# The gate-weight casts and the distance table move behind token tile 2 on ScalarE

## The chip, the cores and the metric

The kernel runs on one core of one Trainium2 chip. The metric is the device time of one execution in microseconds (us), given as the median over several executions. Engines are named as in the profile: PE is TensorE's matmul, PEld its weight loads, DVE is VectorE, ACT is ScalarE, POOL is GpSimd, SP is the engine whose queue issues most DMAs.

## What is computed

One encoder layer on a sequence of S = 1024 tokens of width D = 1024, all in float32:

```python
h = rmsnorm(x, g_mix)
z = h @ w_in                         # pooling channels | q | k | v, 8 heads
y_pool = pool_mixer(u_pool, ...)     # windows 2, 4, 8, 16: mean - self, per-group map
y_attn = diff_attention(q, k, v)     # p1 - lam * p2, bias -slope * |i - j|, chunk mask
gates = sigmoid(h @ w_gate + b_gate)
x = x + (gated sum of the two branch projections) @ w_out
x = x + (relu(rmsnorm(x, g_ffn) @ w_up) ** 2) @ w_down      # 4096 wide
```

Two pieces matter here. `h @ w_gate` (1024 x 2048) needs nothing but `h`, so its matmuls can fill PE while head 0 of the attention is being prepared. And the table of distances |i - j| is built once and is first needed by the attention scores.

## The kernel before

**Precision.** Each float32 operand is held as two rounded parts, high and low. `split` makes them: ACT casts the high part (L132) and DVE or POOL subtracts it from the source for the low part (L133). `mm3` then issues three matmuls, high x high, high x low and low x high (L153, L154, L155), so a logical product of 128 rows is three instructions on PE. Everything is a stream of such triples, with transposes between them (L291 for the normed tokens, L498 for q and k, L1162 for the MLP's input).

**The start.** The 1024 tokens are eight tiles t of 128. Each one is loaded (`load_x`, L333), squared and summed on ACT (L280, key `sq`t), scaled on DVE after a power on POOL (L261, L262, L284, tiles `hn`), transposed on PE into two banks `hps_0`, `hps_1` of four blocks each (L291) and split into `hT`, in four pieces kp = 0 to 3: the casts have the keys `T`t kp `h`, the subtracts `T`t kp `l`. So `T21h` and `T23h` are the casts of pieces 1 and 3 of token tile 2. In the rows below, `hT_<half of the tokens>_<0 high, 1 low>_<number>` carries them; numbers 169 to 175 (even ones low) are pieces 0 to 3 of tiles 0 to 3, and 339 to 345 those of tiles 4 to 7. With `hT` of a tile complete, head 0's projection of it runs: 24 matmuls into `z_t` (L153 to L155), whose squares (ACT L473) lead to the q/k norm (DVE L476, POOL L477, DVE L480) and whose v part is split into `V`. Then q and k are transposed (`tk`, L498) and copied out.

**Fill work.** Between these, `gate_step` feeds PE with the gate projection. `gate_cols(c)` (L780 on) takes 128 columns of `w_gate`: `fill_w` loads them in two halves (SP queue, L711, tiles `frgate`), casts them on ACT into `fwgate` (L132) and subtracts on POOL (L133); then 24 matmuls of 512 tokens each make `g`c`_0`, 24 more `g`c`_1`, and ACT adds the bias (`go`, L785) and stores. `distances` makes an integer table on POOL, takes the absolute value on ACT (L414, tile `dist`, 128 x 1024) and masks a corner on POOL (L415). `columns` transposes a few rows of parameters (`cols_ps`, L419) and copies them on DVE (L420, L421).

**What sets the order.** The order of each engine's instructions is fixed when the program is built. A scheduler runs the program in a timing model and appends to each engine whatever is ready there and ranks first; each engine then works through its list in order, and an instruction that has to wait holds up all behind it. By hand, the tables `FIRST_ACT`, `FIRST_DVE` and `FIRST_PE` (L49 to L58) chain some of the first instructions: `in_turn` walks the keys of a table and makes each instruction follow the one before in issue order, without a wait between engines. A key is looked up in `marks`, where `split` and the norm code have entered their instructions.

**The end.** After the output projection, `norm_token` normalises each token tile for the MLP; for the last one the elementwise part is on POOL (L1146 to L1159, tile `y`), and PE transposes it in two banks `hb_0`, `hb_1` (L1162). The up projection begins before that is done. It combines halves of tokens and weights so that fewer products are needed: products `X`, `Y`, `Z`, `W` of sums `AS`, `B`, `BT` (made on DVE, L1074 and L1077, from the weights `wu`, which the SP queue loads, and split on ACT and DVE), copies on ACT into `x` (L1298), `U` (L1325, L1335) and `z` (L1330), and sums `u` on DVE (L1304) that ACT squares (L1305, L1306).

Of the kernel before, what the change touches and what calls it, by code (L numbers as in the profile page):

```python
# [11 lines left out]
AF = mybir.ActivationFunctionType  # L12
# [35 lines left out]
N_GP = 1  # L48
FIRST_ACT = (  # L49
    "sq0 gc0 gc1 w0h w1h w2h T00h w3h w4h T02h T01h w5h w6h T03h w7h "  # L50
    "sq1 sq2 zq00 T10h T12h sq3 T11h sq4 V00h T20h lx T13h T22h T21h T23h zq01 V01h T30h T32h"
)
FIRST_DVE = (
    "hn00 hn01 w2l T00l w3l T02l T01l w6l T03l w7l rs1 hn10 hn11 rs2 zr00 gg lp T10l hn20 hn21 "
    "ls T12l rs3 T11l rs4 V00l qn00 T20l nl T13l T22l hn30 hn31 hn40 hn41 T21l T23l zr01 V01l T30l T32l"
)
FIRST_PE = "z00 tr10"
# [11 lines left out]
def encoder_kernel(  # L69
# [21 lines left out]
    nc = tc.nc  # L91
# [27 lines left out]
    def ut(shape, dt, name):  # L119
        return up.tile(shape, dt, tag="U", name=name)  # L120
# [4 lines left out]
    def f(ap):  # L125
        return ap.bitcast(F32)

    marks = {}

    def split(hi, lo, src, lo_eng=None, key=None):  # L130

        a = nc.scalar.copy(hi, src)  # L132
        b = (lo_eng or nc.vector).tensor_tensor(lo, src, f(hi), op=ALU.subtract)  # L133
        if key:
            marks[key + "h"], marks[key + "l"] = a.ins, b.ins
        return b

    def queue_behind(ins, first):
        tc.add_manual_dep(
            ins, first.name,  # L140
            mybir.DependencyInfo(mybir.DependencyClass.NoSync, mybir.DependencyReason.DATA),
            reason="issue order",
        )

    def in_turn(keys):
        keys = keys.split()
        for a, b in zip(keys, keys[1:]):
            queue_behind(marks[b], marks[a])
# [12 lines left out]
    def fw_tile(shape, name):  # L161
        return wpool.tile(shape, F32R, tag="fw", name=name, bufs=N_FW)
# [4 lines left out]
    def fr_tile(shape, name):  # L167
        return fp.tile(shape, F32, tag="fr", name=name, bufs=N_FR)
# [140 lines left out]
    with ExitStack() as ph:  # L309
# [6 lines left out]
        def s1(shape, dt, name, tag, bufs=1):  # L316
            return sq_pool.tile(shape, dt, tag=tag, name=name, bufs=bufs)
# [90 lines left out]
        dist = s1([P, S], F32, "dist", "dist")  # L408

        def distances():  # L410

            di = ut([P, S], I32, "di")
            nc.gpsimd.iota(di, pattern=[[-1, S]], base=S - P, channel_multiplier=1)
            nc.scalar.activation(dist, di, AF.Abs)  # L414
            nc.gpsimd.memset(dist[0:64, S - 64 : S], MASKED)  # L415

        def columns():
# [259 lines left out]
        for g in range(-2, N + 8):  # L677
            for t in range(4, NT):
                if LX[t] == g:
                    load_x(t)  # L680
            for t in range(1, NT):
                if NX[t] == g:
                    norm_x(t)
            if g == G_DIST:
                distances()
            if g == G_COLS:
                columns()
            gens = {}
            for tok in ORDER:
                if tok not in gens:  # L690
                    i = g - tok[1]
                    gens[tok] = stage(tok[0], i) if 0 <= i < N else iter(())
                here = tc.cur_priority
                if tok[0] in "HR" and i == N - 1:
                    tc.cur_priority += LATE
                next(gens[tok], None)
                if tc.cur_priority > here + LATE // 2:
                    tc.cur_priority -= LATE
            for gen in gens.values():
                for _ in gen:  # L700
                    pass


    for keys in (FIRST_ACT, FIRST_DVE, FIRST_PE):
        in_turn(keys)

    def fill_w(src, c0, name):
        ws = []
        for j in range(2):
            rw = fr_tile([P, 4, P], f"fr{name}_{j}")  # L710
            nc.sync.dma_start(  # L711
                rw, src[j * 512 : (j + 1) * 512, c0 : c0 + P].rearrange("(kk p) c -> p kk c", p=P)
            )
            w = fw_tile([P, 2, 4, P], f"fw{name}_{j}")
            stored["lo"] = split(w[:, 0], w[:, 1], rw, nc.gpsimd).ins
            ws.append(w)
        return ws

# [21 lines left out]
    def pool_group(g):  # L740
        win = WINDOWS[g]
        ws = fill_w(w_in, g * P, f"pool{g}")
        rg = fr_tile([P, P], f"rgrp{g}")
        nc.sync.dma_start(rg, w_pool_grp[g])
# [35 lines left out]
    def gate_cols(c):  # L780
        ws = fill_w(w_gate, c * P, f"gate{c}")
        for th in range(2):
            ps = fill_proj(ws, th, f"g{c}_{th}", spare_bank if c >= G_Z else fill_bank)
            fo = fo_tile(f"go{c}_{th}")
            nc.scalar.activation(fo[:, 0:512], ps, AF.Identity, bias=cols[:, c : c + 1])  # L785
            nc.scalar.dma_start(g_dram[c * P : (c + 1) * P, th * 512 : (th + 1) * 512], fo[:, 0:512])
            yield
# [8 lines left out]
    stored = {}  # L796
# [62 lines left out]
    while gate_step():  # L859
        pass  # L860
    assert not units_left

    vpool = attn.enter_context(tc.tile_pool(name="vpool", bufs=1))
    pb = mix.enter_context(tc.tile_pool(name="pb", bufs=5, space=PSUM))
# [750 lines left out]
```

## Time and profile before

| | |
|---|---|
| median of 3 runs | 1527.21 us (1526.54 to 1527.58) |
| the profiled execution | 1530.36 us, of which the span of the engines 1528.6 us |
| granted TensorE clock, mean | 0.999 |
| PE busy | 1515.5 us, 99% of the span, 7457 instructions |
| PEld, DVE, ACT, POOL busy | 85%, 64%, 50%, 21% of the span |
| mean DMA traffic | 155 GB/s |

The profiled execution took 3.15 us more than the median; 1.76 us of its time lie outside the span. A timeline row reads: start in us, duration of the group in us, engine, line, operation, output and inputs by the program's names, partitions x elements, and how many instructions the row joins; in square brackets the engine's idle time before it and what ended that. Matmuls are pipelined, so the time that one costs is read from start to start, not from its duration. A windows row gives a stretch, its length, each engine's busy time with the number of instructions, the granted clock as a fraction (PEclk), the busy share of the DMA engines and GB/s.

### The profile page before, as it was taken

What the parts mean: (1) busy time and instruction counts of PE and PEld (TensorE: products, weight loads), DVE (VectorE), ACT (ScalarE), POOL (GpSimd) and SP (SyncE); (2) the same over time, 40 slices, a digit from 0 to 9 for tenths busy, and PEclk for the clock granted to TensorE, in tenths of its full rate; (3) what the DMA queues carried; (4) which work ended last, traced back from release to release, by engine and by line L of the source; (5) the groups of instructions that cost most, each with busy time, mean ns of one, the idle gap of its engine ahead of it and who ended that gap; (6) DMA issues with size and microseconds to landing.
All of it is one profiled execution on the core that took longest, in us unless ns stands there. A gap on an engine that the chain in (4) does not pass through costs nothing.

```text
span 1528.6 us, 21995 instructions
## 1 busy us (share of the span) xinstructions
PE 1515.5 (99%) x7457; PEld 1306.0 (85%) x7457; DVE 979.3 (64%) x2071; ACT 757.6 (50%) x1567; POOL 325.6 (21%) x413
## 2 busy tenths in 40 slices
PE   8999999999999999999999999999999999999999
PEld 6999999999999999888888887888888888888887
DVE  6666566667666666646578569666665668556572
ACT  6545455545454454454464456555555634333331
POOL 5677433334344342212100120000000000000000
PEclk9999999999999999999999999999999999999999
DMA  7455323223232342727366634454433799537650
GB/s 233 125 167 166 105 63 87 68 82 89 68 92 77 90 131 70 248 89 240 133 213 208 226 117 148 153 181 152 142 134 111 268 326 403 172 124 262 227 193 28
DMA packets 195163, 237.36 MB, mean 155 GB/s; under 512 B 13974, under 2 KB 124523, under 8 KB 195052
## 3 DMA queue, kind: packets, MB, share of 16 engines
q1 hardware_dynamic: 177642, 208.66, 42.2%
q10 hardware_dynamic: 17410, 27.31, 4.7%
q8 instruction: 59, 0.97, 0.3%
q14 instruction: 52, 0.43, 0.1%
HBM read 157.24 MB, written 61.90 MB: 143 GB/s over the span
## 4 chain that ended last, share of the span: by engine, by line
PE 93%; DVE 2%; DMA 2%; ACT 1%; SPq 1%; issue 0%; ACTq 0%; DVEq 0%
PE z L153 6%; PE z L155 6%; PE z L154 6%; PE g L154 4%; PE g L155 4%; PE g L153 4%; PE Da L153 4%; PE Da L154 4%; PE Da L155 4%; PE Db L154 3%; PE Db L155 3%; PE Db L153 3%; PE X L153 2%; PE X L155 2%; PE X L154 2%; PE sc L535 2%
## 5 line engine op out<-in xcount | busy, mean ns | idle before, releaser
L153 PE MATMUL z<-wqkv,hT 128*128 128x384 f32 x512 | 176.6, 345 | 2.5 <-ACT hT L132 2.4
L154 PE MATMUL z<-wqkv,hT 128*128 128x384 f32 x512 | 175.6, 344 | 0.0
L155 PE MATMUL z<-wqkv,hT 128*128 128x384 f32 x512 | 174.8, 342 | 0.1
L546 ACT ACTIVATE s<-s,nm 128x256 f32<-128x256 f32 (+7 forms) x128 | 99.5, 778 | 62.2 <-DVE nm L538 61.4
L153 PEld LDWEIGHTS z<-wqkv,hT 128*128 128x128 f32 x512 | 97.6, 191 | 6.0 <-ACT hT L132 3.3
L153 PE MATMUL g<-hT,fwgate 128*128 128x512 f32 x256 | 100.6, 393 | 0.4 <-ACT hT L132 0.4
L155 PE MATMUL g<-hT,fwgate 128*128 128x512 f32 x256 | 101.0, 394 | 0.0
L154 PE MATMUL g<-hT,fwgate 128*128 128x512 f32 x256 | 100.9, 394 | 0.0
L155 PEld LDWEIGHTS z<-wqkv,hT 128*128 128x128 f32 x512 | 97.4, 190 | 2.8 <-DVE hT L133 0.6
L154 PEld LDWEIGHTS z<-wqkv,hT 128*128 128x128 f32 x512 | 97.6, 191 | 2.2
L477 POOL TENSOR_TENSOR ms<-ms,mhalf 128x4 f32<-128x4 f32 x64 | 69.2, 1081 | 138.3 <-DVE ms L476 137.8
L538 DVE CUSTOM_DVE_ANT_0 s<-sc,dist 128x512 f32<-128x512 f32 (+3 forms) x128 | 73.9, 584 | 38.4 <-PE sc L536 38.2
L133 DVE TENSOR_TENSOR AT<-ta,AT 128x256 fp32r<-128x256 f32 (+1 forms) x160 | 61.2, 392 | 47.8 <-ACT AT L132 47.4
L132 ACT CAST AT<-ta 128x256 fp32r<-128x256 f32 (+1 forms) x160 | 54.1, 349 | 50.0 <-PE ta L578 32.4
L133 DVE TENSOR_TENSOR AS<-s,AS 128x512 fp32r<-128x512 f32 x64 | 45.0, 704 | 37.7 <-ACT AS L132 37.6
L535 PE MATMUL sc<-K,Q 128*128 128x512 f32 (+2 forms) x192 | 68.1, 357 | 0.3 <-DMA Q<-Q 0.3
L536 PE MATMUL sc<-K,Q 128*128 128x512 f32 (+2 forms) x192 | 65.7, 347 | 0.0
L133 POOL TENSOR_TENSOR wqkv<-rqkv,wqkv 128x384 fp32r<-128x384 f32 x60 | 62.0, 1051 | 8.5 <-ACT wqkv L132 7.6
L133 POOL TENSOR_TENSOR fwgate<-frgate,fwgate 128x512 fp32r<-128x512 f32 x32 | 42.7, 1336 | 68.8 <-ACT fwgate L132 58.7
L153 PEld LDWEIGHTS g<-hT,fwgate 128*128 128x128 f32 x256 | 48.1, 188 | 8.9 <-ACT hT L132 0.7
L155 PEld LDWEIGHTS g<-hT,fwgate 128*128 128x128 f32 x256 | 48.1, 188 | 8.7
L154 PEld LDWEIGHTS g<-hT,fwgate 128*128 128x128 f32 x256 | 48.1, 188 | 8.5
(472 smaller groups left out, 4379.8 us busy)
## 6 DMA issues: line engine op xcount, KB each, us to landing
wd<-in_w_down_dram SPq DMA_DIRECT2D x56, 512.0 KB, 5.7
wu<-in_w_up_dram SPq DMA_DIRECT2D x32, 512.0 KB, 4.6
udS<-us SPq DMA_DIRECT2D x64, 256.0 KB, 2.1
ur<-udS SPq DMA_DIRECT2D x32, 512.0 KB, 3.4
rqkv<-in_w_in_dram SPq DMA_DIRECT2D x64, 192.0 KB, 2.7
ud<-u ACTq DMA_DIRECT2D x48, 256.0 KB, 3.0
ur<-ud SPq DMA_DIRECT2D x24, 512.0 KB, 7.3
frgate<-in_w_gate_dram SPq DMA_DIRECT2D x32, 256.0 KB, 2.7
```

Of the source, the lines that this page charges most:

```text
L132: a = nc.scalar.copy(hi, src)
L133: b = (lo_eng or nc.vector).tensor_tensor(lo, src, f(hi), op=ALU.subtract)
L153: nc.tensor.matmul(ps, lhs_hi, rhs_hi, start=first, stop=False, **kw)
L154: nc.tensor.matmul(ps, lhs_hi, rhs_lo, start=False, stop=False, **kw)
L155: return nc.tensor.matmul(ps, lhs_lo, rhs_hi, start=False, stop=last, **kw).ins
L477: nc.gpsimd.tensor_tensor(ms, ms, mhalf[:, 0:4], op=ALU.pow)
L535: nc.tensor.matmul(dst, Q[:, 1, i, :], rhs, start=True, stop=False)
L536: nc.tensor.matmul(dst, Q[:, 0, i, :], rhs, start=False, stop=True)
L538: nc.vector.tensor_tensor_reduce(out=s[i][:, c : c + w], in0=sc[:, 0:w], in1=dist[:, o0 + c : o0 + c + w], scale=2.0 ** -(h + 1), scalar=B ...
L546: nc.scalar.activation(s[i][:, 0:n], s[i][:, 0:n], AF.Exp, bias=last, scale=-1.0, accum_out=Z[:, i, t : t + 1])
```

## The change

Two keys become known to the table of ACT: the absolute value of the distance table gets `di`, and the two casts of a gate's weight columns get `gate`c`0h` and `gate`c`1h` (and the subtracts on POOL `...l`, which no table uses). In `FIRST_ACT`, `di` is put behind `T23h`, and the two casts of the first gate columns behind `zq01`, the squares of `z_1`. Since the gate steps create their instructions later in the program text than the tables were applied, the loop over `in_turn` moves behind them.

```diff
@@ -48,7 +48,7 @@
 FIRST_ACT = (
     "sq0 gc0 gc1 w0h w1h w2h T00h w3h w4h T02h T01h w5h w6h T03h w7h "
-    "sq1 sq2 zq00 T10h T12h sq3 T11h sq4 V00h T20h lx T13h T22h T21h T23h zq01 V01h T30h T32h"
+    "sq1 sq2 zq00 T10h T12h sq3 T11h sq4 V00h T20h lx T13h T22h T21h T23h di zq01 gate00h gate01h V01h T30h T32h"
 )
@@ -411,7 +411,7 @@
             nc.gpsimd.iota(di, pattern=[[-1, S]], base=S - P, channel_multiplier=1)
-            nc.scalar.activation(dist, di, AF.Abs)
+            marks["di"] = nc.scalar.activation(dist, di, AF.Abs).ins
@@ -701,9 +701,6 @@
-    for keys in (FIRST_ACT, FIRST_DVE, FIRST_PE):
-        in_turn(keys)
-
     def fill_w(src, c0, name):
@@ -712,7 +709,7 @@
             w = fw_tile([P, 2, 4, P], f"fw{name}_{j}")
-            stored["lo"] = split(w[:, 0], w[:, 1], rw, nc.gpsimd).ins
+            stored["lo"] = split(w[:, 0], w[:, 1], rw, nc.gpsimd, f"{name}{j}").ins
@@ -859,6 +856,9 @@
     assert not units_left
+
+    for keys in (FIRST_ACT, FIRST_DVE, FIRST_PE):
+        in_turn(keys)
```

**ACT at the start.** The difference of ACT's list where the tables apply; a row with a minus stands there before, one with a plus now. `fwgate_0`, `fwgate_1` are the two halves of the first gate weights, `hps_0_294` and `hps_1_304` the transposed token tile 2.

```order
 L132 CAST hT_0_0_173<-hps_1_304 128x2x128
+L132 CAST hT_0_0_171<-hps_0_294 128x2x128
+L132 CAST hT_0_0_175<-hps_1_304 128x2x128
+L414 ACTIVATE dist<-di 128x1024
+L473 ACTIVATE sq<-z_1_449 128x4x64
 L132 CAST fwgate_0_6508<-frgate_0_6506 128x512
 L132 CAST fwgate_1_6513<-frgate_1_6511 128x512
-L414 ACTIVATE dist<-di 128x1024
-L132 CAST hT_0_0_171<-hps_0_294 128x2x128
-L132 CAST hT_0_0_175<-hps_1_304 128x2x128
-L473 ACTIVATE sq<-z_1_449 128x4x64
 L132 CAST V_0_377<-z_1_449 128x128
```

The casts `T21h` and `T23h`, the distance table and the squares of `z_1` have changed places with the two gate casts.

**PE before the second half of the tokens.** The scheduler, which follows from that order, places the gate products otherwise. Before, the end of `g_0` stands between `z_3` and the transposes that lead to `z_4`:

```order
L154 MATMUL g_0_6516<-hT_0_1_176,fwgate_1_6513 128x512
L155 MATMUL g_0_6516<-hT_0_0_175,fwgate_1_6513 128x512
L291 MATMUL hps_1_564<-identf,hn_547 128x128 x4
L498 MATMUL tk_0_513<-identf,qn_0_446 128x128 x2
L291 MATMUL hps_0_554<-identf,hn_547 128x128 x4
L153 MATMUL z_4_662<-wqkv_0_207,hT_1_0_339 128x384
```

In the changed program `z_3` and one small transpose stand there:

```order
L154 MATMUL z_3_598<-wqkv_7_230,hT_0_0_175 128x384
L155 MATMUL z_3_598<-wqkv_7_230,hT_0_1_176 128x384
L419 MATMUL cols_ps<-identf,rows 128x32
L291 MATMUL hps_1_564<-identf,hn_547 128x128 x4
L498 MATMUL tk_0_513<-identf,qn_0_446 128x128 x2
L291 MATMUL hps_0_554<-identf,hn_547 128x128 x4
L153 MATMUL z_4_662<-wqkv_0_207,hT_1_0_339 128x384
```

All 24 products of `g_0` now stand between `z_2` and `z_3`, where they were mixed with `z_3` and with transposes before. The number of instructions on PE is the same. On DVE, `hn_547` and what follows it to the subtract `T61l` (row `hT_1_1_342<-hps_0_481`) are the same eight steps in another order.

**The beginning of the MLP.** Two places of the late program move too. On PE the two groups of transposes of the last token tile go further back, the first behind five products, the second behind seven; five products stand between them, where there were three. This is the first of the two:

```order
-L1162 MATMUL hb_0_10099<-identf,y_9835 128x128 x4
 L154 MATMUL X_10159<-B11l,A_1_10161 128x512
 L155 MATMUL X_10159<-B11h,A_1_10161 128x512
 L153 MATMUL X_10159<-B11h,A_1_10161 128x512
-L1162 MATMUL hb_1_10100<-identf,y_9835 128x128 x4
 L154 MATMUL X_10159<-B11l,A_1_10161 128x512
 L155 MATMUL X_10159<-B11h,A_1_10161 128x512
+L1162 MATMUL hb_0_10099<-identf,y_9835 128x128 x4
```

Both banks have moved away from the place at which PE met them, and the products passed over need only weights and tokens that were there.

And on ACT, some 25 us later, the copies `U_0` and `z_0` come ahead of the cast of a weight tile that is still being loaded (`A_5`):

```order
 L132 CAST A_4_10698<-wu_0_10694 128x512
-L132 CAST A_5_10858<-wu_0_10854 128x512
 L132 CAST AS_1_10500<-s_1_10460 128x512
-L132 CAST A_1_10523<-wu_1_10454 128x512
 L1325 COPY U_0_10358<-X_10116 128x512
 L1330 COPY z_0_10376<-Z_10360 128x512
+L132 CAST A_5_10858<-wu_0_10854 128x512
+L132 CAST A_1_10523<-wu_1_10454 128x512
```

Before, the copy `U_0` stood behind that cast. Nothing in the diff touches this part of the program: the scheduler's choices there follow from its whole run.

## The prediction

> **What bounds the kernel now.** I read the page's busy times first, then the waits of PE, then the timelines around the places where the order changed.
>
> ```profile
> span 1528.6 us, 21995 instructions
> PE 1515.5 (99%) x7457; PEld 1306.0 (85%) x7457; DVE 979.3 (64%) x2071; ACT 757.6 (50%) x1567; POOL 325.6 (21%) x413
> ...
> PE z L153 <- ACT hT L132: 2.4, 2, 1.6
> PE hb L1162 <- POOL y L1159: 2.0, 2, 1.0
> PE X L153 <- ACT U L1325: 0.9, 1, 0.9
> PE g L153 <- ACT hT L132: 0.4, 1, 0.4
> ```
>
> PE is busy for all but 13.1 us of the span, so the bound is its list of instructions. A change that adds and removes no work there can bring only what PE waits, what a lower clock costs, and what the order of unlike instructions costs. The four waits shown (total, number, longest) are those that stand near a changed row; they sum to 5.7 us. Three are in the rows that follow, with their places.
>
> **The start: what is removed.** ACT's timeline, then PE's, around the first gate casts:
>
> ```profile
> 24.78 1.37 ACT L132 CAST fwgate<-frgate 128x512 fp32r<-128x512 f32 x2 [3.05 <-DMA frgate<-in_w_gate_dram]
> 26.06 1.05 ACT L414 ACTIVATE dist<-di 128x1024 f32<-128x1024 int32 x1
> 27.02 0.62 ACT L132 CAST hT<-hps 128x256 fp32r<-128x256 f32 x2
> ```
> ```profile
> 24.82 1.03 PE L291 MATMUL hps<-identf,hn 128*128 128x128 f32 x8
> 27.43 0.45 PE L153 MATMUL z<-wqkv,hT 128*128 128x384 f32 x1 [1.58 <-ACT hT L132]
> ...
> 28.41 0.50 PE L153 MATMUL g<-hT,fwgate 128*128 128x512 f32 x1 [0.36 <-ACT hT L132]
> ...
> 30.28 0.52 PE L153 MATMUL z<-wqkv,hT 128*128 128x384 f32 x1
> 30.60 0.52 PE L154 MATMUL z<-wqkv,hT 128*128 128x384 f32 x1
> ```
>
> ACT stands 3.05 us on the load of the gate weights, although the casts `T21h` and `T23h`, behind it in its list, read a bank that PE had filled long before. They run at 27.02, after 1.37 of gate casts and 1.05 of the distance table, and PE idles 1.58 and then 0.36 for them. In the new order both casts run in ACT's idle time, from about 21.8, the distance table and the squares of `z_1` fill some more of the 3.05, and the gate casts still start at 24.78 when their load lands. PE's 1.58 + 0.36 = 1.94 us fall away. The low parts of these pieces come from DVE, which is busy to 25.2 with the norm of tiles 3 and 4 and then free, in time for 25.85, when PE's transposes end.
>
> Behind that gap the clock falls:
>
> ```profile
> 25.74:29.15 3.41, 1.47 (x9) 0.96 (x8) 1.75 (x6) 3.41 (x9) 3.41 (x5) 1.00 0.92 348
> 29.15:32.57 3.42, 3.42 (x14) 3.42 (x13) 2.66 (x8) 2.85 (x8) 2.13 (x4) 0.54 0.46 139
> 916.54:919.95 3.41, 2.25 (x11) 1.27 (x10) 3.41 (x6) 2.38 (x5) 3.41 (x2) 1.00 0.10 38
> ```
>
> The window after the gap has a granted clock of 0.54, and products of 384 columns follow each other by 0.32 us (30.28, 30.60) where at full clock it is 0.18 (37.40 and 37.58, quoted next). Over 3.42 us that is 3.42 x (1 - 0.175/0.32) = 1.55 for products alone, and 1.70 with the group of transposes that straddles the end. A window like the third, with PE busy for 2.25 of 3.41, kept its clock; the first, with 1.47, did not. With the gap gone, the first has PE full, so I take the clock to stay up and **1.70** back (bounds 0 and 1.70).
> The Trainium skill ("TensorE: Matmul & The Clock Gate", on the HAM clock gate and its oscillation) has the clock halved after an idle window of about 3.4 us and says "no PE-idle gaps >~3.4µs"; as worded, 1.58 idle would not do it, and the 1.70 would stay. The rows disagree with the letter of it: a gap of less than half that stands right before the only 0.54 here. I keep the other way as rival C.
>
> **The order of groups.** Transposes cost more than themselves:
>
> ```profile
> 36.79 0.60 PE L291 MATMUL hps<-identf,hn 128*128 128x128 f32 x4
> 37.14 0.42 PE L155 MATMUL z<-wqkv,hT 128*128 128x384 f32 x1
> 37.40 0.34 PE L153 MATMUL z<-wqkv,hT 128*128 128x384 f32 x1
> 37.58 0.34 PE L154 MATMUL z<-wqkv,hT 128*128 128x384 f32 x1
> ```
>
> The first product behind a group takes 0.26 from start to start, the others 0.18, so each change of kind costs about 0.09. Between `z_2` and `z_4` the list now has 4 places with transposes where there were 9; 5 x 0.09 = **0.45**. Gross gain at the start: 1.94 + 1.70 + 0.45 = 4.1.
>
> **The start: what is added.** Without the products of `g_0` between `z_3` and the second half's first transposes, what these need is due earlier:
>
> ```profile
> 39.01 1.06 ACT L280 ACTIVATE hn<-x 128x1024 f32<-128x1024 f32 x1
> ...
> 41.08 1.42 DVE L284 SCALAR_TENSOR_TENSOR hn<-x,rs,gmb 128x512 f32<-128x512 f32 x2 [0.19 <-POOL rs L262]
> ...
> 43.88 0.74 DVE L133 TENSOR_TENSOR hT<-hps,hT 128x256 fp32r<-128x256 f32 x2
> ...
> 46.92 0.44 PE L153 MATMUL z<-wqkv,hT 128*128 128x384 f32 x1
> ```
>
> From the start of `hn_547` to the end of `T61l` DVE takes 41.08 to about 44.3, 3.2 us without a pause, for the same steps as in the new order, and `hn_547` starts 2.07 behind its square (39.01). In the new order that square stands behind the casts of tile 5's transposes, which PE reaches after 6 of `z_3`'s 24 products. PE would end `z_3` at about 45.5 - 4.1 = 41.4; counted back (24 products of 0.175, four groups of 0.35), those transposes end near 37.1, the casts near 37.8, so `hn_547` starts near 39.9 and `T61l` ends near 43.1. The transposes in `hps_0` need it, since it empties their bank, and PE would be there at 42.0: a new wait of **1.1**. `z_4` then needs the bank that `qn_2` empties, two DVE steps of about 0.37 behind `T61l`, at 43.9, where PE comes at 43.7: **0.2**. Both are estimates, 1.3 together; 0.3 if the square comes a us earlier than worked out, 2.0 if it comes 0.7 later, since DVE's chain then moves with it.
>
> One more load comes due earlier, the tokens of tile 4 (SP's issue, ACT's square of that tile, and the time to landing of such loads):
>
> ```profile
> 23.33 1.01 SPq L333 DMA_DIRECT2D x<-in_x_dram  x2
> ...
> x<-in_x_dram SPq DMA_DIRECT2D x4, 512.0 KB, 4.3
> ```
> ```profile
> 29.54 1.09 ACT L280 ACTIVATE hn<-x 128x1024 f32<-128x1024 f32 x1
> ```
>
> Issued at 23.33 and with a median of 4.3, it lands between 27.6 and the 29.54 at which it was used. Pulled ahead on ACT, the square may stand there for it, and the casts of tile 3 behind it, whose products PE wants next: 0 to 0.6, I take **0.3**. The net gain at the start is 4.1 - 1.1 - 0.2 - 0.3 = **2.5**; bounds 0.8 (half clock stays) and 3.8 (no `T61l` wait).
>
> **The MLP's beginning.** PE, then ACT:
>
> ```profile
> 918.45 0.66 PE L1162 MATMUL hb<-identf,y 128*128 128x128 f32 x4 [1.00 <-POOL y L1159]
> ...
> 919.17 0.39 PE L155 MATMUL X<-B11h,A 128*128 128x512 f32 x1
> 919.39 0.40 PE L153 MATMUL X<-B11h,A 128*128 128x512 f32 x1
> 920.76 0.66 PE L1162 MATMUL hb<-identf,y 128*128 128x128 f32 x4 [0.97 <-POOL y L1159]
> ...
> 947.32 0.50 PE L153 MATMUL X<-BT3h,AS 128*128 128x512 f32 x1 [0.94 <-ACT U L1325]
> ```
> ```profile
> 945.12 0.62 ACT L132 CAST A<-wu 128x512 fp32r<-128x512 f32 x1 [3.19 <-DMA wu<-in_w_up_dram]
> ...
> 946.69 0.57 ACT L1325 COPY U<-X 128x512 f32<-128x512 f32 x1
> ```
>
> POOL's pieces `y` are ready at 918.45 and 920.76. From start to start the two waits cost 1.17 and 1.14 above a product of 0.227, together 2.3. With five products ahead of the first transposes (5 x 0.227 = 1.14) PE comes to them at 918.4, no wait; five more between the groups bring it to the second at about 920.1, 0.7 early. So 2.3 - 0.7 = **1.6** come back. Later, `U_0` stands behind a cast that waits 3.19 for a weight load; ahead of it, it can be done by about 942.5, two us before PE wants its bank, and **0.9** come back. Against that, `Z_1` now waits on a DVE sum (`u`) that is at the end of a full queue; I take **-0.2**. Net 2.3. The lower bound is 0, from the same DVE:
>
> ```profile
> 910.00:930.00 20.00, 18.03 (x85) 14.49 (x84) 19.98 (x31) 14.03 (x28) 7.63 (x5) 1.00 0.42 131
> 930.00:950.00 20.00, 19.06 (x85) 15.44 (x84) 19.54 (x32) 12.89 (x24) 0.00 (x0) 1.00 0.44 133
> ```
>
> It is busy for 39.5 of these 40 us, so PE, coming earlier, may find the operands that DVE makes not there, and wait for them instead. Two things speak for most of the gain all the same: PE waits for no DVE result in this stretch before, and DVE's own list starts a little earlier there. The upper bound is 2.9, with 0.3 of the second wait left and none on `u`: 2.3 - 0.3 + 0.9.
>
> **Sum.** 2.5 + 2.3 = 4.8. On the profiled execution that is 1528.6 - 4.8 = 1523.8 for the span, or 1525.6 with the 1.76 outside it. That execution lies 3.15 above the median; the waits and the clock are taken to be alike in the timed ones, so the median becomes 1527.21 - 4.8 = **1522.4**.
>
> **The rivals.** *B, only the start pays* (1527.21 - 2.5 = 1524.7): DVE, full over the 40 us, sets the MLP's beginning, and the waits at L1162 and on `U` return as waits for `AS` or `u`. For it the two windows; against it that PE's only waits there name POOL and ACT. *C, the half clock is not the gap's* (4.8 - 1.7 = 3.1, 1524.1): it comes at a time of its own, or the new wait of 1.1 + 0.2 near 42 brings another. For it that one occurrence proves no cause; against it that 1.3 is less than the 1.94 of the window that lost the clock. *D, slower*: the second gate columns.
>
> ```profile
> 26.77 8.73 SPq L711 DMA_DIRECT2D frgate<-in_w_gate_dram  x4
> ```
> ```profile
> 31.29 0.62 ACT L132 CAST fwgate<-frgate 128x512 fp32r<-128x512 f32 x1 [0.57 <-DMA frgate<-in_w_gate_dram]
> ```
>
> Their load is issued when POOL has released a buffer, and landed at 31.29. The cast of it now stands ahead of the squares of `z_2`, a `V` and the casts of tile 4, on which the transposes of `z_3`'s stretch hang. It holds PE up only if it lands later than about 36.5, each us beyond that costs one, and the gain of the start and the end is spent at 41.3; to lose 3.8 it has to land near 45, giving 1531. The buffer's release hangs on the gate casts, which keep their time at 24.78, so 5 us are to spare; against D. *E, no change* (1527): the late choices of the scheduler cancel and the start's gain turns into the wait at `T61l`.
>
> **How the numbers follow.** A measurement of this kernel tells about 0.2%, 3 us, from no change. The forecast with both places has 0.58, B 0.14, C 0.14, D 0.08, E 0.06. Within the forecast the gain is 3.1 to 6.5, nearly always over 3 (0.55 of the 0.58); of B 0.03 and of C 0.04 are over it. Faster 0.62; same 0.03 + 0.11 + 0.10 + 0.06 = 0.30; slower 0.08. The range runs from 1520.0 (all upper bounds but some of the new waits) to 1526.5 (B or C with the start at its lower side), leaving out D, half of E and the rims.
>
> **What would show it.** In PE's waits the rows `z <- ACT hT` and `X <- ACT U` are gone and `hb <- POOL y` is one wait of about 0.7; a wait for a DVE `hT` (L291) of about 1 us appears near 42. The window at 29.15 has a clock of 1.00. ACT's gate casts still start near 24.8, and `z_4` starts near 44.3 instead of 46.92. In the stretch of the MLP's beginning PE comes 2.3 nearer. The prediction is wrong if half clock shows up again between 25 and 50, if PE waits on `AS` or `u` behind 920 for over a us, or if `z_3` waits for a cast behind the gate load.

## The result and the profile after

The changed kernel takes 1524.15 us (median of 19 runs, 1523.14 to 1525.55), the kernel before in the same sessions 1527.38 us (19 runs, 1526.04 to 1529.48). The ratio is 0.9977 with a 95% interval of 0.9971 to 0.9983: 3.5 us faster (2.6 to 4.4), at the edge of what a measurement here tells from no change. Forecast were 1522.4 in a range of 1520.0 to 1526.5, and a gain of 4.8 us, which lies outside 2.6 to 4.4. The spans of the two profiled executions differ by exactly those 4.8 (1528.6 and 1523.8), which is no confirmation: the profiled execution of the kernel before took 1530.36, 3.0 us above its median, that of the changed one 1525.54, 1.4 above.

The waits of the changed kernel's PE (total, how often, the longest):

```profile
PE hps L291 <- DVE hn L284: 1.2, 1, 1.2
PE z L153 <- ACT hT L132: 0.8, 1, 0.8
PE Db L153 <- ACT w_0h L132: 0.6, 1, 0.6
PE hps L291 <- DVE hT L133: 0.5, 1, 0.5
PE hb L1162 <- POOL y L1159: 0.5, 1, 0.5
PE X L155 <- DVE AS L133: 0.2, 1, 0.2
```

The first two stand at the very start, ahead of the changed rows (the second profile of the kernel before, below, has both). Gone are the 1.58 and 0.36 on `hT` at 27 us and the 0.94 on `U`; the two waits on `y` have become one of 0.5. New are 0.5 on `hT` L291, which is the bank that `T61l` empties, 0.2 on `AS`, and 0.6 on `w_0h`, far behind the change at 1258 us.

ACT at the start of the changed kernel (timeline), then PE there, then the two windows after the first token tiles, each with its busy times in the order PE, PEld, DVE, ACT, POOL and its granted clock in the third column from the end:

```profile
22.86 1.06 ACT L414 ACTIVATE dist<-di 128x1024 f32<-128x1024 int32 x1
25.08 0.38 ACT L473 ACTIVATE sq<-z 128x256 f32<-128x256 f32 x1 [1.16 <-PE z L155]
25.36 1.13 ACT L132 CAST fwgate<-frgate 128x512 fp32r<-128x512 f32 x2
```
```profile
25.17 1.47 PE L291 MATMUL hps<-identf,hn 128*128 128x128 f32 x12
26.40 0.42 PE L155 MATMUL z<-wqkv,hT 128*128 128x384 f32 x1
...
42.90 0.66 PE L291 MATMUL hps<-identf,hn 128*128 128x128 f32 x4 [0.53 <-DVE hT L133]
43.56 0.44 PE L153 MATMUL z<-wqkv,hT 128*128 128x384 f32 x1
```
```profile
25.74:29.15 3.41, 3.41 (x26) 3.38 (x25) 1.66 (x6) 3.41 (x9) 3.10 (x3) 1.00 0.54 201
29.15:32.57 3.42, 3.42 (x18) 2.91 (x17) 3.14 (x7) 3.29 (x12) 3.42 (x6) 1.00 0.39 114
```

ACT no longer waits for the load: by 25.36 the weights are there, and what it waits for is `z_1`, whose squares stand ahead of the gate casts now. So these start 0.6 us later than before (24.78) and not at the same time, as was forecast; the first product that needs them comes at 29.71. PE runs without a pause from `z_1` into `z_2`, the clock stays at 1.00, and `z_4` starts at 43.56 instead of 46.92.

The beginning of the MLP in the changed kernel's timeline, PE and then ACT:

```profile
914.62 0.66 PE L1162 MATMUL hb<-identf,y 128*128 128x128 f32 x4
...
916.93 0.66 PE L1162 MATMUL hb<-identf,y 128*128 128x128 f32 x4 [0.51 <-POOL y L1159]
...
941.25 0.39 PE L153 MATMUL X<-BT3h,AS 128*128 128x512 f32 x1
```
```profile
938.57 0.57 ACT L1325 COPY U<-X 128x512 f32<-128x512 f32 x1
...
941.68 1.14 ACT L132 CAST A<-wu 128x512 fp32r<-128x512 f32 x2 [2.04 <-DMA wu<-in_w_up_dram]
```

The first transposes meet a finished `y`, the second wait 0.51, and `U` is copied two us before its bank is wanted, ahead of the cast that waits for `wu`. Taking PE's instructions of the two traces in list order, the changed kernel is ahead by 3.4 us at `z_4`, 3.8 before the MLP, 5.9 at 955 us, and 4.8 from 1265 us to the end: 1.1 are lost again at `w_0h`.

### The profile page after: what moved, and what is told of

Read it like the earlier page. It is cut to its first block, busy times and chain, and to the rows that moved or that the text cites. A ratio compares the mean times of both kernels' runs of the same rounds, so it can differ in the third digit from the quotient of the medians.

```text
span 1523.8 us, 21991 instructions
## 1 busy us (share of the span) xinstructions
PE 1513.8 (99%) x7457; PEld 1304.2 (86%) x7457; DVE 980.4 (64%) x2071; ACT 757.3 (50%) x1567; POOL 327.6 (21%) x413
## 3 DMA queue, kind: packets, MB, share of 16 engines
q1 hardware_dynamic: 177642, 208.66, 42.4%
## 4 chain that ended last, share of the span: by engine, by line
PE 92%; DVE 3%; DMA 2%; ACT 1%; issue 1%; POOL 0%; SPq 0%; ACTq 0%; DVEq 0%; POOLq 0%
PE z L153 6%; PE z L155 6%; PE z L154 6%; PE g L155 4%; PE g L154 4%; PE g L153 4%; PE Da L153 3%; PE Da L154 3%; PE Da L155 3%; PE Db L154 3%; PE Db L155 3%; PE Db L153 3%; PE X L155 2%; PE X L153 2%; PE X L154 2%; PE sc L536 2%
## 5 line engine op out<-in xcount | busy, mean ns | idle before, releaser
L486 POOL TENSOR_TENSOR qn<-qn,ggh 128x128 f32<-128x128 f32 x64 | 33.7, 526 | 105.8 <-DVE qn L480 89.1
L155 PEld LDWEIGHTS g<-hT,fwgate 128*128 128x128 f32 x256 | 48.1, 188 | 8.8
L154 PEld LDWEIGHTS g<-hT,fwgate 128*128 128x128 f32 x256 | 48.1, 188 | 8.5
```

Of the source, the lines that this page charges most:

```text
L154: nc.tensor.matmul(ps, lhs_hi, rhs_lo, start=False, stop=False, **kw)
L155: return nc.tensor.matmul(ps, lhs_lo, rhs_hi, start=False, stop=last, **kw).ins
L486: nc.gpsimd.tensor_tensor(qn[:, :, 1, :], qn[:, :, 1, :], ggh.unsqueeze(1).broadcast_to([P, 2, HD]), op=ALU.mult)
```

## The experiments

All were timed in alternation with the kernel before; each also left a profile. The ratio is to the kernel before of the same session.

| run | what | ratio (95%) |
|---|---|---|
| again | the kernel before | 1.0001 (0.9993 to 1.0010) |
| late_only | only the order of the MLP's beginning | 0.9989 (0.9980 to 0.9998) |
| di_only | only the distance table moved | 0.9995 (0.9987 to 1.0004) |
| gates_only | only the gate casts moved | 0.9974 (0.9964 to 0.9983) |
| start_only | only the order of the start | 0.9989 (0.9980 to 0.9998) |
| load_later_before | before, gate load later | 1.0039 (1.0026 to 1.0051) |
| load_later_after | changed, gate load later | 0.9989 (0.9980 to 0.9998) |
| load_early | before's start, gate load earlier, changed end | 0.9980 (0.9971 to 0.9989) |
| after_again | the changed kernel | 0.9971 (0.9960 to 0.9982) |
| t61_early | changed, `T61l` earlier | 0.9973 (0.9963 to 0.9983) |

### The kernel before, once more

Nothing is edited.

> The kernel before, unchanged, timed against itself and profiled once more. In the two profiles at hand the change is worth 4.8 us, in the timed medians 3.2 us, and the profiled execution of the kernel before was 3.0 above its median. Theory 1 (the half clock at 29 us comes only in some executions of the kernel before, since the clock's windows start at another moment in each): this profile may well show a granted clock of 1.0 behind the gap; then z_4 starts near 45.2 instead of 46.9 and the profiled time lies near the median, 1527 to 1528.5. Theory 2 (it comes in every execution, and the 1.6 us between profile and median are something else): the half clock is there again and z_4 starts at 46.9. The ratio is 1.000 within 0.0006 by both.

Its PE in the timeline, then the window that holds the gap:

```profile
25.76 0.44 PE L153 MATMUL z<-wqkv,hT 128*128 128x384 f32 x1
26.04 0.34 PE L154 MATMUL z<-wqkv,hT 128*128 128x384 f32 x1
26.75 0.50 PE L153 MATMUL g<-hT,fwgate 128*128 128x512 f32 x1 [0.37 <-ACT hT L132]
27.87 0.63 PE L291 MATMUL hps<-identf,hn 128*128 128x128 f32 x4 [0.62 <-DVE hT L133]
...
44.54 0.45 PE L153 MATMUL z<-wqkv,hT 128*128 128x384 f32 x1
```
```profile
26.05:29.46 3.41, 2.42 (x14) 1.82 (x14) 3.26 (x8) 2.88 (x7) 3.01 (x5) 1.00 0.71 229
```

No half clock, and not even the gap of 1.58: PE idles 0.37 + 0.62, and `z_4` starts 2.4 us earlier than in the first profile of the same program. The reason stands on ACT:

```profile
23.12 1.38 ACT L132 CAST fwgate<-frgate 128x512 fp32r<-128x512 f32 x2 [1.25 <-DMA frgate<-in_w_gate_dram]
```

The gate load landed 1.7 us earlier than in the first profile (24.78). The earlier load has a price, too: POOL's subtracts of these weights now run at 23.82, beside DVE's norm of tiles 3 and 4, which takes 4.79 us where it took 2.73 in the first profile. The 0.62 is PE's wait for the subtract behind it:

```profile
22.60 4.79 DVE L284 SCALAR_TENSOR_TENSOR hn<-x,rs,gmb 128x512 f32<-128x512 f32 x4
```

So both the size of the gap and the half clock belong to the execution, not to the program. That is theory 1.

### Only the beginning of the MLP

```diff
+    X1, Y1 = marks["X1"], marks["Y1"]
+    seq = X1[11:] + hb7[:4] + Y1[:5] + hb7[4:] + Y1[5:6]
+    for a, b in zip(seq, seq[1:]):
+        queue_behind(b, a)
+    queue_behind(marks["A11_5h"], marks["z5_0"])
```

`X1` and `Y1` are the twelve products of `X_10159` and `Y_10160`, `hb7` the eight transposes of the last tile; a few lines that record them move the helpers' lines by 2 or 3. On PE only the two groups of transposes move; on ACT the cast of `A_5` goes behind the copies, and one subtract of DVE follows it. The changed kernel's lists differ at more places behind these, up to 1035 us, which stay as before here.

> The start is as in the kernel before; only at the beginning of the MLP the order of the change is put in by hand: the two groups of transposes of the last token tile behind the last five products of X and five of Y, and the copies U_0 and z_0 ahead of the cast of A_5. Theory of two separate gains: PE gains 2.2 us between 900 and 950 (the two waits on POOL's y shrink from 2.0 to about 0.5, the wait on U of 0.9 is gone), and the median falls by 2.2, to a ratio of 0.9986, if nothing is given back; by 1.1 (0.9993) if the first products of the down projection's next group (Db on w_0h) wait again for their weight load as they do in the changed kernel. Rival (DVE sets this place): no gain, ratio 1.000, and the waits come back under AS or u. A second thing it tells, as a third profile of the same start: whether the half clock at 29 us is there (theory 2) or not always (theory 1).

The median falls to 1525.97 from 1528.29, the ratio says 1.7 us (0.3 to 3.1). PE's waits of this kernel:

```profile
PE z L155 <- ACT hT L134: 2.3, 2, 1.5
PE X L157 <- DVE A L135: 0.5, 1, 0.5
PE hb L1165 <- POOL y L1162: 0.5, 1, 0.5
```

The waits on `y` are 0.5, that on `U` is gone, and 0.5 on DVE's part of `A` has come. In its trace PE gains 1.9 us on the first profile of before between 900 and 960, where the changed kernel gains 2.1, and nothing is lost at `w_0h`. So the two places named carry nearly all of it, the end's part is real without the start's, and DVE takes a small share of it back, not all. The start of this program is that of the kernel before, a third profile of it; PE's row at the gap, then the two windows around it:

```profile
25.80 0.45 PE L155 MATMUL z<-wqkv,hT 128*128 128x384 f32 x1 [1.47 <-ACT hT L134]
```
```profile
23.02:26.43 3.41, 1.94 (x13) 1.34 (x11) 1.51 (x4) 3.13 (x8) 2.55 (x3) 1.00 0.99 351
26.43:29.85 3.42, 3.05 (x19) 2.95 (x20) 2.66 (x9) 2.71 (x7) 2.67 (x5) 1.00 0.75 246
```

Here the gap is nearly as long as in the first (1.47 + 0.37, against 1.58 + 0.36), and yet the clock stays: the boundary of the clock's windows falls between the two parts, and neither of the two windows has PE busy for less than 1.94. The gap is long although the load landed as early as in the second profile:

```profile
23.18 1.36 ACT L134 CAST fwgate<-frgate 128x512 fp32r<-128x512 f32 x2 [2.75 <-DMA frgate<-in_w_gate_dram]
```

PE came sooner, with the transposes of tile 3 at 23.30 instead of 24.93, since its full clock began 3 us earlier in this execution (last section). The gap is as long as the load is late against PE, and both vary.

### One part alone

Against the table of the changed kernel, on the first line:

```diff
-    "... T21h T23h di zq01 gate00h gate01h V01h T30h T32h"
+    "... T21h T23h di zq01 V01h T30h T32h"              (di_only)
+    "... T21h T23h zq01 gate00h gate01h V01h T30h T32h" (gates_only)
```

> Only the distance table goes behind T21h and T23h; the gate casts stay ahead of them. The beginning of the MLP keeps the order of the kernel before. ACT makes T21h at 26.05 instead of 27.02, but PE now has the products that wait for it ahead of tile 3's transposes, so it idles about 1.4 us from 25.0 to 26.4 and comes to the next products 0.4 to 0.5 us earlier than before. If the clock falls behind a gap by where the windows lie, 1.4 us in one piece cost 1.7 or nothing: gain 0.5 where the kernel before had full clock, 2.2 where it had half. Median 1526.9 to 1525.2, ratio 0.9997 to 0.9986; theory 1 says near the first, theory 2 near the second. Rival (the distance table alone is what matters): 3 us, 0.998.

> Only the gate casts go behind zq01; the distance table stays ahead of T21h. Orders of PE, DVE, POOL and SP are those of the changed kernel; on ACT the table comes two casts earlier, in time that ACT spends idle. Theory: same as the changed kernel, ratio 0.9979, z_4 at 43.6, PE 5.9 ahead of the kernel before near 950, and it is the gate casts alone that carry the change. Rival (both parts are needed): T21h comes a us later, PE idles 0.5 to 1 us near 26 and the gain falls to 2.2 or less. It is also a second profile of the changed order: if the 1.1 us that were given back at the first Db near 1258 hang on the landing of single loads, the wait for w_0h there may be another (0 to 1.2); if they hang on the order, it is 0.6 again and PE's lead falls from 5.9 to 4.8.

gates_only is the whole change: 0.9974. With its table go the changed lists of PE, DVE, POOL and SP, the end's included; di_only keeps the end of the kernel before. di_only is 0.9995, not told from no change; its PE idles 0.35 at 24.74, because the load landed at 23.04 in this execution too. The expectation of 1.4 there was made for the late load of the first profile. In this one trace `z_4` starts at 43.00, no later than in the changed kernel; the end's waits are those of before. That the distance table alone is worth 3 us is excluded.

In gates_only there is no wait on `w_0h`, though its end has the changed order, and di_only has one of 0.5 with the order before.

### The start alone

From here on every engine's list is written out as a chain of issue order, without waits of its own, so that only what is named differs:

```diff
         encoder_kernel(tc, *args)
+        _in_this_order(nc, tc)
```

> Every engine's list is written out: up to the middle of the program it is that of the changed kernel, from there on (the beginning of the MLP and all behind it) that of the kernel before. Theory of two separate gains, with the half clock left out: the start gives 1.0 to 1.9 (PE's idle time at 26 us was 1.0 in the second profile of the kernel before and 1.9 in the first, less 0.5 for the new wait on T61l, plus about 0.5 of other things in head 0), the MLP's beginning nothing; ratio 0.9990 (0.9987 to 0.9994), waits on POOL's y 2.0 and on U 0.9 as before. If the half clock sat in most executions of the kernel before: 0.9978. If the start gives nothing: 1.000.

Measured 0.9989, as forecast without the half clock, and 0.9978 would be the forecast with it in most executions. Its waits at the end are those of the kernel before:

```profile
PE hb L1162 <- POOL y L1159: 2.0, 2, 1.0
PE X L153 <- ACT U L1325: 1.3, 1, 1.3
```

start_only and late_only together make 0.9989 x 0.9989 = 0.9978, the change 0.9977: two gains of about 1.7 us each that add, as far as intervals of 0.0009 to either side can tell.

### The load later, in both orders

```diff
-frgate_0, frgate_1, wq_0 (2 pieces), x_406, x_408
+wq_0 (2 pieces), x_406, x_408, frgate_0, frgate_1
```

(SP's list of loads; all else as named.)

> All lists are those of the kernel before, but on SP the two loads of the first gate columns go behind four others (two pieces of a branch weight and two token tiles), so they are issued about 2.5 us later. Theory (in the order before, PE's gap at 26 us is as long as the load is late, since T21h and T23h stand behind it on ACT): the gap grows by 2.4 to 3 us to about 4, z_4 starts 2.4 to 3 later, and a half clock of one window (1.7) becomes likely. Ratio 1.0016 to 1.0030. Rival (the gap hangs on something else, such as the distance table or DVE): less than 1 us, ratio 1.000.

> The same delay of the same loads, with all other lists as in the changed kernel. Theory (the changed order takes PE off that load): ACT waits 1 to 2 us for the load near 25.5, but PE has z_2 to do until 29.5; loss against the changed kernel 0 to 0.5, ratio to the kernel before 0.9977 to 0.9982. Rival (whoever needs the gates waits as long as the load is late): 2.4 us, ratio 0.9993.

In the order before, ACT, PE, and the windows around the gap:

```profile
27.86 1.36 ACT L132 CAST fwgate<-frgate 128x512 fp32r<-128x512 f32 x2 [6.80 <-DMA frgate<-in_w_gate_dram]
```
```profile
30.49 0.69 PE L153 MATMUL z<-wqkv,hT 128*128 128x384 f32 x1 [5.35 <-ACT hT L132]
```
```profile
24.25:27.66 3.41, 0.90 (x9) 0.66 (x7) 0.27 (x1) 0.00 (x0) 0.00 (x0) 1.00 0.81 276
27.66:31.07 3.41, 0.58 (x2) 0.50 (x2) 0.60 (x2) 3.08 (x8) 2.52 (x3) 0.50 0.04 12
31.07:34.49 3.42, 3.42 (x12) 2.83 (x11) 2.66 (x8) 3.42 (x10) 2.82 (x6) 0.50 0.53 155
```

ACT and with it DVE and POOL stand still (0.27 and 0.00 of 3.41), PE idles 5.35 us in one piece, and two windows run at half clock. The kernel loses 6.0 us (4.0 to 7.8), more than the 2.4 to 4.6 expected, since the load landed 4.7 later than in the second and third profile, not 2.5.

In the changed order, with the same delay, ACT and PE:

```profile
27.21 1.37 ACT L132 CAST fwgate<-frgate 128x512 fp32r<-128x512 f32 x2 [3.29 <-DMA frgate<-in_w_gate_dram]
```
```profile
29.07 0.49 PE L153 MATMUL g<-hT,fwgate 128*128 128x512 f32 x1 [0.73 <-ACT hT L132]
31.96 0.50 PE L153 MATMUL g<-hT,fwgate 128*128 128x512 f32 x1 [1.00 <-ACT hT L132]
```

The loss is 1.8 us against the change (0.9989 instead of 0.9977; by the two intervals 0.2 to 3.5), where 0 to 0.5 were expected and 2.4 by the rival. In the trace PE waits 0.73 + 1.00, and not for the weights: `g_0` takes all 512 tokens of the first half, and the casts of token tile 3 stand behind the gate casts on ACT. The changed order has put more of PE's work between itself and the load; it has not made PE independent of it.

### The load earlier

```diff
-rqkv_0 (2 pieces), rqkv_1 (2 pieces), frgate_0, frgate_1
+frgate_0, frgate_1, rqkv_0 (2 pieces), rqkv_1 (2 pieces)
```

The lists of the start are those of the kernel before, those of the end the changed ones.

> The start's lists are those of the kernel before, ACT's included, the lists from the MLP's beginning on those of the changed kernel; on SP the loads of the first gate columns go ahead of four weight loads of the next head, so they are issued 2 to 3 us earlier. Theory (the cause is the load's lateness, the order of ACT is one cure of two): the wait of ACT on the load is gone, PE's idle time at 26 us falls under 0.4, z_4 starts near 43.5 without the new wait on T61l, and with the 2.2 of the MLP's beginning the kernel is as fast as the changed one or up to 0.5 faster: ratio 0.9977 (0.9973 to 0.9982). Rival (the order of PE's products at the start is what helps, by fewer changes between transposes and products): it stays at the 2.2 of the end, 0.9986.

0.9980, within what was expected; the end alone (late_only) has 0.9989, and the interval of 0.9971 to 0.9989 holds the rival's 0.9986 too. ACT waits for no gate load any more, but a wait stands in the gap's place all the same (ACT, then PE):

```profile
21.34 1.19 ACT L132 CAST fwgate<-frgate 128x512 fp32r<-128x512 f32 x2
```
```profile
27.96 0.63 PE L291 MATMUL hps<-identf,hn 128*128 128x128 f32 x4 [1.77 <-DVE hT L133]
```

DVE is late. Its work ahead of that `hT` is four `hn` steps, here beside POOL's subtracts of the gate weights and a product behind them (1.17 us); the first row is DVE, the second POOL:

```profile
22.21 5.27 DVE L284 SCALAR_TENSOR_TENSOR hn<-x,rs,gmb 128x512 f32<-128x512 f32 x4
```
```profile
22.37 3.43 POOL L133 TENSOR_TENSOR fwgate<-frgate,fwgate 128x512 fp32r<-128x512 f32 x2
```

In the first profile of the kernel before, and in the changed one, DVE does the same four ahead of the gate casts, while POOL subtracts nothing (changed kernel):

```profile
22.48 2.73 DVE L284 SCALAR_TENSOR_TENSOR hn<-x,rs,gmb 128x512 f32<-128x512 f32 x4
```

5.27 against 2.73, so the earlier load swaps one wait for another of 1.77, and `z_4` starts at 44.63, where 43.5 was expected. The gap has two causes, then: a late load holds `T21h` on ACT, as theory has it, and an early one brings POOL's subtracts beside DVE's norm and so holds the low parts on DVE (0.62 in the second profile of the kernel before). The order of ACT takes both away: with the gate casts behind `z_1`, the four `hn` steps take 2.73 to 2.89 in all six profiles that have this order. In time the two cures are not told apart, nor is the rival (fewer changes between transposes and products) excluded as a part of the start's gain: the early load makes 0.9980 / 0.9989 = 0.9991 beside the end's part, the order of ACT 0.9989 (start_only).

### The changed kernel again, and its one new wait

```diff
 ACT   hT_1_0_343<-hps_1_491
-      sq<-z_3, V_0<-z_3, hT_1_0_341<-hps_0_481
+      hT_1_0_341<-hps_0_481, hT_1_0_345<-hps_1_491, sq<-z_3, V_0<-z_3
 DVE   cols
-      ms_3, V_0, gs, T61l, hT_1_1_344<-hps_1_564, qn_2, T63l
+      T61l, qn_2, T63l, ms_3, V_0, gs, hT_1_1_344<-hps_1_564
```

(t61_early; after_again has no edit.)

> The changed kernel, once more. Ratio to the kernel before 0.9977 within 0.0009. Its second profile shows what is of the order and what of one execution: the wait for T61l (0.5) and one wait on POOL's y (0.5) are there again and no half clock; if the wait for w_0h at 1258 (0.6, with which PE's lead fell from 5.9 to 4.8) is a matter of how single loads land, it may be missing as it was in two other runs with this order of the end; if it is of the order, it is there again.

> All lists are those of the changed kernel, but on ACT the casts T61h and T63h go ahead of the squares of z_3 and its V, and on DVE the subtract T61l and qn_2 go ahead of ms_3, V and gs. Theory (the one wait that the change added at the start, 0.53 for T61l and some 0.2 behind it, is only the order of those small steps): T61l ends at 42.2 instead of 42.8, the wait of the transposes in hps_0 is under 0.1, z_4 starts near 43.0 instead of 43.56, and the kernel is 0.5 to 0.7 us faster than the changed one: ratio to the kernel before 0.9973, which the timing alone can hardly tell from 0.9977. Rival (hn_547's own lateness holds PE there): z_4 does not move.

after_again measured 0.9971. It has the same 0.53 at `T61l` and the same 0.5 on `y`, and no wait on `w_0h`: PE's lead over the first profile of the kernel before is 6.8 us at 960 us and 6.7 at the end, where it fell to 4.8 in the first profile. (1.4 of the 6.7 it had already at the transposes of tile 3, from an earlier full clock.) That loss belonged to one execution.

PE of t61_early, timeline:

```profile
42.24 0.66 PE L291 MATMUL hps<-identf,hn 128*128 128x128 f32 x4
42.75 0.44 PE L498 MATMUL tk<-identf,qn 128*128 128x128 f32 x2
43.20 0.66 PE L291 MATMUL hps<-identf,hn 128*128 128x128 f32 x4
43.71 0.44 PE L153 MATMUL z<-wqkv,hT 128*128 128x384 f32 x1
```

From the first transposes to `z_4` it is 1.47 us, in the changed kernel 41.42 to 43.56, 2.14: the wait is gone and 0.67 with it, by a reordering of small steps alone. In the same execution PE waited 1.1 for `g_0`, so `z_4` itself was late. The gate weights were there; this time the squares of token tile 4 held up the casts of tile 3 on ACT:

```profile
29.74 1.06 ACT L280 ACTIVATE hn<-x 128x1024 f32<-128x1024 f32 x1 [2.09 <-DMA x<-in_x_dram]
```

In after_again ACT waited 1.13 for the same tokens, without a wait of PE; in the first profile of the changed kernel it did not wait. The median (0.9973) cannot show 0.7 us, and whether t61_early beats the changed kernel is left open.

## Why the prediction was right, and which of its terms was not

**Sign, place and both mechanisms held.** ACT's wait for the gate load is what held `T21h` back: moved later, the load costs the old order 6.0 us and the new one 1.8; moved earlier, ACT's wait is gone. And the end's part comes from the two moved groups of transposes and the moved copies: late_only has it without the start.

**The mis-sized term is the clock's 1.70**, "with the gap gone ... I take the clock to stay up and 1.70 back". It was there in one of three profiles of the kernel before's start. Every fall of the clock that was seen followed a gap of PE, but not every such gap brought one: it matters how much of the gap falls into one window of the clock. The granted clock of the first profile rises at 15.74 us, falls at 29.39 and rises at 32.81: four windows of 3.41 and one. The last window before the fall, the one behind it, and a window of load_early:

```profile
25.98:29.39 3.41, 1.60 (x9) 1.20 (x10) 1.94 (x6) 3.41 (x9) 3.41 (x5) 1.00 0.91 345
29.39:32.81 3.42, 3.42 (x12) 3.36 (x11) 2.70 (x7) 2.85 (x9) 2.13 (x4) 0.50 0.41 123
25.74:29.15 3.41, 1.64 (x12) 1.36 (x11) 3.41 (x8) 2.48 (x5) 1.87 (x4) 1.00 1.00 352
```

In the first profile PE was busy for 1.60 of 3.41, and the next window ran at half. With 0.90 and 0.58 (load_later_before) the clock fell or stayed down; with 1.94 (late_only), 2.42 (again) and 1.64 (load_early, 1.77 idle in one piece) it stayed up. So the limit lies near 1.6 by this measure. It is not shown that PE's busy time is exactly what counts: the ends of matmuls are modelled, 1.60 and 1.64 are close, and the last window of late_only (1518.06 to 1521.47), also with 1.60, was followed by no fall. The windows lie differently in each execution (the first rise is at 12.78 to 15.81 us in the twelve traces), so a gap of 1.8 us costs half a window's work (1.7 us) or nothing, by chance. The sentence "the waits and the clock are taken to be alike in the timed ones" was the wrong step. Rival C's price, 4.8 - 1.7 = 3.1 or 1524.1, is what was measured (3.2 by medians), though not for its reason that the half clock comes by itself.
The Trainium skill ("TensorE: Matmul & The Clock Gate", Part 1, "What's actually happening") calls this window free-running and run-variable; the boundaries here agree, with first rises at 12.78 to 15.81 us. Its wording for the fall, an idle window of about 3.4 us, the rows do not bear out: 1.8 us idle inside one window was enough once.

**The gap's 1.94** was the size of one execution as well. It was 0.99 in the second profile, where the load landed at 23.12 instead of 24.78, and 1.84 in the third, where it landed at 23.18 but PE came 1.6 us sooner. The row of 2.4 in PE's waits was read too widely: 0.8 of it stands at 9.83 us, before the first product of `z_0`, far ahead of every changed row, and is there after the change as well.

**The new waits, 1.1 + 0.2 + 0.3 = 1.6, were set too high.** `T61l` costs 0.53 and not 1.1: it ended near 42.8 and not 43.1 (`hn_547` started at 39.72 instead of 39.9, and DVE took 3.1 for the chain), and PE came to the transposes in `hps_0` at 42.4 and not 42.0. The wait for the tokens of tile 4 did not come in the profile of the change; in t61_early it came and cost PE 1.1, more than the bound of 0.6. By profiles, the start is worth 3.4 us against the first profile of before, which is the gross 4.1 less 0.7; counted from the place where PE's lists part (24.82 in the changed kernel) to `z_4`, it is 0.9 against the second profile (no half clock, early load) and 1.8 against the third. Timed alone it is 1.7 (0.3 to 3.1), where 2.5 stood in the sum. That 2.5 still lies in this interval is partly luck: a gain that two of three profiles do not have and waits set too high cancel in part. The 4.8 us between the two profiled spans are luck too: they are 3.4 at the start, 0.4 behind it, 2.1 at the MLP's beginning, less the 1.1 lost at `w_0h`.

**The MLP's beginning**: 2.3 were forecast, 2.1 appear in the trace of the change and 1.9 in late_only; timed alone it is 1.7 (0.3 to 3.1). The second wait on `y` was forecast at 0.7 and is 0.5; `U` came back in full; DVE took 0.2 (0.5 in late_only).

**Rivals.** B fell: DVE is as full as before at this place, and PE gained all the same (the changed kernel's windows there, taken 5 us earlier since PE is ahead by that; DVE is the third of the busy times):

```profile
905.00:925.00 20.00, 19.49 (x95) 15.82 (x94) 20.00 (x31) 13.37 (x26) 8.09 (x6) 1.00 0.34 100
925.00:945.00 20.00, 19.85 (x88) 16.12 (x87) 19.07 (x32) 14.05 (x28) 0.00 (x0) 1.00 0.44 139
```

PE is now busy for 39.3 of 40 us, where it was 37.1. D fell: PE never waited for the second gate load (its cast ran at 30.21 without a pause; in start_only ACT waited 0.83 for the second half of it, and PE did not). E fell with start_only and late_only.

**What stays open:** how often the half clock comes in timed executions, which carry no trace; one of three profiles had it. Whether the early load or the order of ACT is the better cure, and what part of the start's gain the fewer changes between transposes and products make (0.45 in the sum). And whether t61_early's 0.7 us is a gain of the whole.

## What to carry to other kernels

One profile is one execution: before a wait or a clock step of a us or two goes into a sum, see in a second profile of the same program whether it is there, and compare the profiled time with the median (3.0 us above it here was the hint). An engine that runs its list in order should not have a cast that waits for a load ahead of casts whose inputs are long there; how much that costs shows best by making the load later in both orders (6.0 against 1.8 us here). That an input comes early is not free either: here it set POOL to work beside DVE and slowed both. And a scheduler that plans the whole program moves rows far from the edit, so read the order at every place where PE waits: half of this gain came 880 us behind the edit.

## What the runs showed of the hardware

The start of full clock varies as well: the granted clock rises at 12.78 us in late_only and at 15.81 in again, and the spacing of PE's products goes from 0.32 to 0.17 us there. At 20 us late_only's PE is 1.5 us ahead of again's, in the same list; part of this the later gap takes back (0.7 are left at `z_4`). How much of the kernel before's spread of 3.4 us it makes was not separated.

DVE's `hn` step, which reads two tiles from SBUF, took 0.68 us alone (four in 2.73) and 1.3 beside POOL's work in load_early (four in 5.27); POOL's two subtracts took 2.50 alone and 3.43 beside it. The Trainium skill ("SBUF — State Buffer", on the two sides of SBUF) has a port pair that DVE and GpSimd hold exclusively, for DVE steps with two SBUF inputs too; the rows agree in sign. One behind the other, DVE's four, POOL's two subtracts and its product (0.73 alone) would take 2.73 + 2.50 + 0.73 = 5.96; DVE's four were through in 5.27.
